# Products of 512 moving columns made as two products of 256, in a two-layer decoder trunk

## The chip, the cores and the metric

The kernel runs on one core of one Trainium2 chip. The metric is the device time of one execution in microseconds (us); the time of a kernel is the median of its runs. TensorE is the engine of the matrix products (PE in the profile, PEld for its weight loads), VectorE is DVE, ScalarE is ACT, GpSimd is POOL and SyncE is SP.

## What is computed

The reference is a trunk of two layers on an input of 256 rows by 2048 columns, all in 32-bit floats. Each layer is a mixer and a squared-ReLU MLP, both behind a norm and with a residual. Cut to what matters here:

```python
D_MODEL, SEQ, DEPTH, D_FF = 2048, 256, 2, 8192
h = x
for layer in range(DEPTH):
    u = rms_norm(h, norm_mix) @ w_in            # 2048 -> 6160 (layer 0) or 7176 (layer 1)
    mix = concat(mixer_a(u), mixer_b(u)) @ w_out    # 2048 -> 2048
    h = h + mix
    h = h + square(relu(rms_norm(h, norm_mlp) @ w_up)) @ w_down   # 2048 -> 8192 -> 2048
return rms_norm(h, final_norm)
```

The mixers (gated linear attention and MoBA in layer 0, FoX and HGRN2 in layer 1) are small beside the four projections.

## The kernel before, in words

Every projection is cut into `Block`s of 1024 output columns (1040 or 1032 in one block of each input projection, `extra` 16 or 8). A block runs over its contraction rows in steps of 128; a step is one unit `i`, with row tile `j` in its block. `fetch` brings the weight rows of a unit by DMA (two units to a transfer of 1 MB), and splits them: ScalarE rounds them to `wh` (line 1001), VectorE makes the remainder `wl` (line 1002). The other operand is split in the same way (`xh`, `xl` for the normed input, `mh`, `ml` for the mixer's output and for the MLP's hidden rows), so each product of the reference is a sum of three: high by high, high by low, low by high.

`step(t, i)` issues the products of unit `i` for the `t`-th half of the 256 rows of x. The main loop issues step 0 of unit `i` and step 1 of unit `i - 2`, and then gives small tasks of the mixers (transposes, scores, attention) a share of the queues by `bg`. A step works in one of two ways:

- Input, output and down projections (line 1045): the stationary operand is a 128x128 piece of `xh`, `xl`, `mh` or `ml`, and the moving operand is a piece of `wh` or `wl`. A block's sums stand in two banks of PSUM of 512 columns each, `acc{t}0` and `acc{t}1` (`b.cuts`). A block with extra columns has cuts of 512 and twice 264 or 260 columns, the last in a bank `aux`. A product is one `matmul` over the columns of one bank.
- Up projections (`turned`, line 1028): the weights are stationary, 128 columns at a time, and the 256 rows of `xh` or `xl` are the moving operand. Two sums of 256 columns stand in one bank, and the flag `start` is given only with the first.

Within a step of the first kind the products go part by part, and in each part bank by bank, so that products next to each other share their stationary operand; in the first and the last step of a block they go bank by bank, so that the first bank is done early and can be read (`b.evac`) while the second is still summed. Each `matmul` of the program becomes a weight load and a product on TensorE, also where the stationary operand is that of the one before. The order on each engine is that of the program except that a scheduler moves instructions a little by what it expects of their times; `pin` holds the first 14 units as written.

Of the kernel before, what the change touches and what calls it, by code (L numbers as in the profile page):

```python
# [38 lines left out]
def trunk(ctx: ExitStack, tc: tile.TileContext, x, ev_norm_mix, ev_w_in, ev_gla_gate_w2, ev_gla_gate_b,  # L39
# [3 lines left out]
    pe, act, dve, pool = nc.tensor, nc.scalar, nc.vector, nc.gpsimd  # L43
# [35 lines left out]
    def until(cond):  # L79
        n = 0  # L80
        while not cond():
            bg(10.0, 10.0)
            n += 1
            assert n < 1000
        state["credit"] = min(state["credit"], 0.0)


    def aux():
        state["aux"] += 1
        return psum.tile([P, 512], F32, name="aux", tag="aux", bufs=NAUX)  # L90

    def aux_done():
        state["aux"] -= 1
# [174 lines left out]
    def pin(op):  # L268

        if state["start"]:  # L270
            tc.keep_in_program_order(op)
# [733 lines left out]
    def step(t, i, end=None):  # L1005

        b, j = units[i]
        n = len(b.rows)
        if not b.ready(j):
            until(lambda: b.ready(j))  # L1010
        if j == 0:
            accs[t] = [psum.tile([P, 512], F32, name=f"acc{t}{c}", tag=f"acc{t}{c}")[:, 0:b.cuts[c][1] - b.cuts[c][0]]
                       for c in range(2)]
            if b.extra:
                accs[t].append(aux()[:, 0:b.cuts[2][1] - b.cuts[2][0]])
        banks = accs[t]
        if b.turned:
            assert end is None
            wh, wl = split[i]
            sh, sl = b.stat(j)  # L1020
            parts = [(wh, sh), (wl, sh), (wh, sl)]
            fs = [(o, k) for o in range(2) for k in range(2)]
            order = [(f, p) for f in fs for p in range(3)] if j in (0, n - 1) else [(f, p) for p in range(3) for f in fs]
            for (o, k), p in order:
                m, a = parts[p]
                c0 = t * 512 + (o * 2 + k) * P

                pe.matmul(banks[o][:, k * S:(k + 1) * S], m[:, c0:c0 + P], a, start=j == 0 and p == 0 and k == 0,  # L1028
                          stop=j == n - 1 and p == 2 and k == 1, skip_group_check=True)
            if j == n - 1:  # L1030
                b.evac(banks, t)
            return
        ts = slice(t * P, (t + 1) * P)
        parts = []
        for ii in range(i, end or i + 1):
            jj = units[ii][1]
            wh, wl = split[ii]
            sh, sl = b.stat(jj)
            parts += [(sh[:, ts], wh, jj == 0, False), (sh[:, ts], wl, False, False), (sl[:, ts], wh, False, jj == n - 1)]
            j = jj  # L1040
        outs = list(zip(banks, b.cuts))

        order = [(o, p) for o in outs for p in parts] if j in (0, n - 1) and i else [(o, p) for p in parts for o in outs]
        for (o, (c0, c1)), (a, m, first, last) in order:
            pin(pe.matmul(o, a, m[:, c0:c1], start=first, stop=last))  # L1045
        if j == n - 1:
            b.evac(banks, t)
            if b.extra:
                aux_done()
# [19 lines left out]
    for i in range(total + LAG):  # L1069
        if i % 2 == 0 and i // 2 + 2 < 8:  # L1070
            load_x(i // 2 + 2)
        if i + AHEAD < total:
            fetch(i + AHEAD)
        state["start"] = i < STARTN
        if i < total:
            step(0, i)
        if i % 2 == 0 and i // 2 + 1 < 8:
            first_norm(i // 2 + 1)
        if i == 4:
            load_vectors()  # L1080
            spawn(vector_task())
            tasks.append(tk_const)
        if i == 12:
            for half in range(2):
                spawn(stats_task("ev_mix", half))
        if LAG <= i < total:
            step(1, i - LAG)
        bg(units[min(i, total - 1)][0].budget)
    step(1, total - LAG, total)
    until(lambda: not tasks)  # L1090

# [29 lines left out]
```

## Time and profile before

| what | value |
|---|---|
| median of 3 runs | 2314.34 us (2314.3 to 2315.16) |
| the profiled execution, its own time | 2313.99 us |
| its span, first to last instruction | 2312.3 us |
| PE busy | 2293.0 us (99% of the span) |
| PEld busy | 2009.5 us (87%) |
| DVE, ACT busy | 1285.3 us (56%), 1086.5 us (47%) |

The span is what the trace shows, and the execution's own time is 1.7 us longer. PE's busy time counts a product from its start to its modelled end, and products overlap, so how fast the products follow each other is read from the distance of their starts, not from the duration of one.

### The profile page before, as it was taken

The page shows a single profiled execution, that of the slowest core. Times are in us where ns is not written, and L with a number is a line of the kernel's source. Part 1 is how long each engine was busy: PE and PEld are TensorE (multiplying, and loading weights), DVE is VectorE, ACT ScalarE, POOL GpSimd, SP SyncE. Part 2 cuts the span into 40 slices and gives each one's busy share as a digit, 9 for nine tenths or more (in the row PEclk, how much of TensorE's full clock was granted, in tenths as well). Part 3 has the DMA queues.
Part 4 walks back from the last instruction along what each step waited for, and adds up shares of the span by engine and source line. Part 5 has one row for each costly group of instructions (what it writes and reads, how often), then busy time and mean ns, then how long its engine had stood idle before and what let it go on. Part 6 is the DMA issues. An engine that isn't in the chain of part 4 may idle for free.

```text
span 2312.3 us, 32691 instructions
## 1 busy us (share of the span) xinstructions
PE 2293.0 (99%) x13652; PEld 2009.5 (87%) x13652; DVE 1285.3 (56%) x1564; ACT 1086.5 (47%) x1370; POOL 62.2 (3%) x136
## 2 busy tenths in 40 slices
PE   8999999999999999999999999999999999999998
PEld 7888888998998998998887888788988988988986
DVE  5575545554554464465557775555554554554554
ACT  5464544443453353354446555544443443443443
POOL 2000100000000000000000000100000000000000
PEclk9999999999999999999999999999999999999999
DMA  7645445555556555555554434455555555565553
GB/s 241 190 155 164 154 156 184 184 198 184 198 185 198 184 198 184 197 186 183 183 181 163 164 128 164 146 182 182 192 192 187 196 187 195 189 194 185 198 185 124
DMA packets 110613, 418.69 MB, mean 181 GB/s; under 512 B 6814, under 2 KB 8944, under 8 KB 110336
## 3 DMA queue, kind: packets, MB, share of 16 engines
q1 hardware_dynamic: 109536, 415.46, 54.5%
q8 instruction: 107, 1.75, 0.3%
q10 hardware_dynamic: 608, 1.06, 0.1%
q14 instruction: 42, 0.34, 0.0%
q0 software_dynamic: 320, 0.07, 0.0%
HBM read 414.47 MB, written 2.10 MB: 180 GB/s over the span
## 4 chain that ended last, share of the span: by engine, by line
PE 97%; ACT 1%; DVE 1%; DMA 0%; SPq 0%; issue 0%; POOL 0%; POOLq 0%; ACTq 0%
PE acc L1045 61%; PE acc L1028 30%; PE aux L438 1%; PE aux L1045 1%; PE aux L277 1%; PE aux L339 1%; DMA raw<-in_ev_w_in_dram 0%; PE aux L516 0%; ACT wh L1001 0%; PE aux L540 0%; DVE wl L1002 0%; PE aux L515 0%; PE aux L431 0%; PE aux L561 0%; PE aux L371 0%; PE aux L560 0%
## 5 line engine op out<-in xcount | busy, mean ns | idle before, releaser
L1002 DVE TENSOR_TENSOR wl<-raw,wh 128x1024 fp32r<-128x1024 f32 (+2 forms) x784 | 960.1, 1226 | 879.4 <-ACT wh L1001 877.3
L1001 ACT ACTIVATE wh<-raw 128x1024 fp32r<-128x1024 f32 (+2 forms) x784 | 830.6, 1061 | 1115.8 <-PE acc L1045 675.2
L1045 PE MATMUL acc<-wh,ml 128*128 128x512 f32 x1280 | 413.7, 394 | 0.0
L1045 PE MATMUL acc<-wl,mh 128*128 128x512 f32 x1280 | 413.0, 393 | 0.0
L1045 PE MATMUL acc<-wh,mh 128*128 128x512 f32 x1280 | 412.6, 393 | 0.0
L1028 PE MATMUL acc<-xh,wh 128*128 128x256 f32 x2048 | 348.8, 277 | 0.0
L1028 PE MATMUL acc<-xl,wh 128*128 128x256 f32 x2048 | 347.9, 277 | 0.0
L1028 PE MATMUL acc<-xh,wl 128*128 128x256 f32 x2048 | 347.9, 277 | 0.0
L1028 PEld LDWEIGHTS acc<-xh,wh 128*128 128x128 f32 x2048 | 287.0, 188 | 2.6
L1045 PEld LDWEIGHTS acc<-wh,ml 128*128 128x128 f32 x1280 | 240.5, 188 | 55.1
L1045 PEld LDWEIGHTS acc<-wl,mh 128*128 128x128 f32 x1280 | 240.4, 188 | 52.7
L1045 PEld LDWEIGHTS acc<-wh,mh 128*128 128x128 f32 x1280 | 238.1, 188 | 55.2 <-DVE stg L897 1.7
L1028 PEld LDWEIGHTS acc<-xh,wl 128*128 128x128 f32 x2048 | 285.2, 188 | 0.7
L1028 PEld LDWEIGHTS acc<-xl,wh 128*128 128x128 f32 x2048 | 285.1, 188 | 0.0
L1045 PE MATMUL acc<-wh,xh 128*128 128x512 f32 x832 | 271.3, 397 | 3.1 <-ACT xh L283 3.1
L1045 PE MATMUL acc<-wl,xh 128*128 128x512 f32 x832 | 262.6, 387 | 2.6 <-DVE wl L1002 2.6
L1045 PE MATMUL acc<-wh,xl 128*128 128x512 f32 x832 | 262.3, 386 | 0.0
L1045 PEld LDWEIGHTS acc<-wl,xh 128*128 128x128 f32 x832 | 152.4, 188 | 34.2 <-DVE wl L1002 4.3
L1045 PEld LDWEIGHTS acc<-wh,xl 128*128 128x128 f32 x832 | 152.8, 188 | 31.0
L1045 PEld LDWEIGHTS acc<-wh,xh 128*128 128x128 f32 x832 | 147.6, 189 | 29.8 <-ACT xh L283 4.0
L872 DVE TENSOR_TENSOR h<-acc,h 128x512 f32<-128x512 f32 x72 | 47.9, 686 | 20.2 <-PE acc L1045 20.2
L897 DVE SCALAR_TENSOR_TENSOR stg<-acc,rrow 128x512 f32<-128x512 f32 x64 | 42.3, 685 | 15.1 <-PE acc L1028 15.1
(241 smaller groups left out, 1005.5 us busy)
## 6 DMA issues: line engine op xcount, KB each, us to landing
raw<-in_ev_w_up_dram SPq DMA_DIRECT2D x64, 1024.0 KB, 5.0
raw<-in_ev_w_down_dram SPq DMA_DIRECT2D x64, 1024.0 KB, 5.5
raw<-in_od_w_up_dram SPq DMA_DIRECT2D x64, 1024.0 KB, 5.0
raw<-in_od_w_down_dram SPq DMA_DIRECT2D x64, 1024.0 KB, 5.5
raw<-in_od_w_in_dram SPq DMA_DIRECT2D x48, 1024.0 KB, 4.9
raw<-in_ev_w_in_dram SPq DMA_DIRECT2D x39, 1024.0 KB, 5.5
raw<-in_ev_w_out_dram SPq DMA_DIRECT2D x16, 1024.0 KB, 5.5
raw<-in_od_w_out_dram SPq DMA_DIRECT2D x16, 1024.0 KB, 5.5
```

The costliest lines, as they stand in the source:

```text
L277: pin(pe.transpose(ps[:, i * 256 + t * P:i * 256 + (t + 1) * P], h[:, t, kt * P:(kt + 1) * P], ident))
L339: pe.transpose(ps[:, i * P:(i + 1) * P], src[:, (n0 + i) * P:(n0 + i + 1) * P], ident)
L438: pe.matmul(ps[:, i * 64:(i + 1) * 64], a, r, start=True, stop=True)
L872: dve.tensor_tensor(h[:, t, sl], acc[i], h[:, t, sl], ALU.add)
L897: dve.scalar_tensor_tensor(y, acc[i].rearrange("p (k s) -> p k s", s=S), 0.0, rr, ALU.max, ALU.mult)
L1001: pin(act.activation(wh, raw, AF.Copy))
L1002: pin(dve.tensor_sub(wl, raw, wh.bitcast(F32)))
L1028: pe.matmul(banks[o][:, k * S:(k + 1) * S], m[:, c0:c0 + P], a, start=j == 0 and p == 0 and k == 0, stop=j == n - 1 and p == 2 and k == 1, ...
L1045: pin(pe.matmul(o, a, m[:, c0:c1], start=first, stop=last))
```

## The change

In `step`, a product whose moving operand has 512 columns is issued as two of 256 columns, with the same stationary operand, next to each other, into the two halves of the same bank. Cuts of 264 and 260 columns stay as they are, and so do the up projections. The flag `start` is given only with the first half of a bank's first product, `stop` only with the last half of its last.

```diff
-        outs = list(zip(banks, b.cuts))
-
-        order = [(o, p) for o in outs for p in parts] if j in (0, n - 1) and i else [(o, p) for p in parts for o in outs]
-        for (o, (c0, c1)), (a, m, first, last) in order:
-            pin(pe.matmul(o, a, m[:, c0:c1], start=first, stop=last))
+
+        outs = [[(o[:, u - c0:v - c0], u, v, u == c0, v == c1) for u, v in
+                 (((c0, c0 + 256), (c0 + 256, c1)) if c1 - c0 == 512 else ((c0, c1),))] for o, (c0, c1) in zip(banks, b.cuts)]
+
+        if j in (0, n - 1) and i:
+            order = [(o, p) for bank in outs for p in parts for o in bank]
+        else:
+            order = [(o, p) for p in parts for bank in outs for o in bank]
+        for (o, u, v, f, e), (a, m, first, last) in order:
+            pin(pe.matmul(o, a, m[:, u:v], start=first and f, stop=last and e, skip_group_check=True))
```

On TensorE, the first step of a block of layer 0's output projection, bank by bank, and the step after it (`mh`, `ml` are the stationary operands; 2646, 2647 and 2718, 2719 are the banks of the two row halves). Before:

```order
1366 L1045 MATMUL acc_2718<-wh,mh_1994 128x512
1367 L1045 MATMUL acc_2718<-wl,mh_1994 128x512
1368 L1045 MATMUL acc_2718<-wh,ml_1995 128x512
1369 L1045 MATMUL acc_2719<-wh,mh_1994 128x512
1370 L1045 MATMUL acc_2719<-wl,mh_1994 128x512
1371 L1045 MATMUL acc_2719<-wh,ml_1995 128x512
1372 L1045 MATMUL acc_2646<-wh,mh_1994 128x512
1373 L1045 MATMUL acc_2647<-wh,mh_1994 128x512
1374 L1045 MATMUL acc_2646<-wl,mh_1994 128x512
1375 L1045 MATMUL acc_2647<-wl,mh_1994 128x512
```

The same place in the changed kernel, where line 1045 has become line 1050:

```order
1367 L1050 MATMUL acc_3792<-wh,mh_2762 128x256 x2
1368 L1050 MATMUL acc_3792<-wl,mh_2762 128x256 x2
1369 L1050 MATMUL acc_3792<-wh,ml_2763 128x256 x2
1370 L1050 MATMUL acc_3793<-wh,mh_2762 128x256 x2
1371 L1050 MATMUL acc_3793<-wl,mh_2762 128x256 x2
1372 L1050 MATMUL acc_3793<-wh,ml_2763 128x256 x2
1373 L1050 MATMUL acc_3690<-wh,mh_2762 128x256 x2
1374 L1050 MATMUL acc_3691<-wh,mh_2762 128x256 x2
1375 L1050 MATMUL acc_3690<-wl,mh_2762 128x256 x2
1376 L1050 MATMUL acc_3691<-wl,mh_2762 128x256 x2
```

Each row has become two products in the same place; nothing stands between the two halves, and the order of banks and parts is the same.

On ScalarE, at the end of the first block of layer 0's input projection (line 628 reads the finished bank `acc_131`, line 1001 rounds weights for later steps). Before:

```order
27 L1001 ACTIVATE wh<-raw 128x1040 x2
28 L628 ACTIVATE stg<-acc_131,rq 128x512
29 L1001 ACTIVATE wh<-raw 128x1040 x2
30 L341 ACTIVATE gqT<-aux 128x4x128
31 L341 ACTIVATE gkT<-aux 128x4x128
```

In the changed kernel:

```order
27 L1001 ACTIVATE wh<-raw 128x1040 x3
28 L628 ACTIVATE stg<-acc_131,rq 128x512
29 L1001 ACTIVATE wh<-raw 128x1040
30 L341 ACTIVATE gqT<-aux 128x4x128
31 L341 ACTIVATE gkT<-aux 128x4x128
```

One rounding of weights has moved ahead of the reading of the bank. Elsewhere on ScalarE and VectorE only single instructions of the mixers and of the weight splits trade places with a neighbour.

## Rows read from the trace of the kernel before

**Rows 1.** The page: span, busy time of each engine, granted clock in 40 slices.

```profile
span 2312.3 us, 32691 instructions
PE 2293.0 (99%) x13652; PEld 2009.5 (87%) x13652; DVE 1285.3 (56%) x1564; ACT 1086.5 (47%) x1370; POOL 62.2 (3%) x136
...
PEclk9999999999999999999999999999999999999999
```

**Rows 2.** The page: the chain that ended last, shares by engine.

```profile
PE 97%; ACT 1%; DVE 1%; DMA 0%; SPq 0%; issue 0%; POOL 0%; POOLq 0%; ACTq 0%
```

**Rows 3.** Waits of PE (what for: us in total, times, longest).

```profile
PE aux L1057 <- DMA vrow<-in_ev_norm_mix_dram: 3.7, 1, 3.7
PE acc L1045 <- ACT xh L283: 3.1, 2, 2.4
PE acc L1045 <- DVE wl L1002: 2.6, 3, 2.2
```

**Rows 4.** Groups of PE's products by form: xcount | busy us, mean ns.

```profile
L1045 PE MATMUL acc<-wh,ml 128*128 128x512 f32 x1280 | 413.7, 394 | 0.0
...
L1028 PE MATMUL acc<-xl,wh 128*128 128x256 f32 x2048 | 347.9, 277 | 0.0
...
L1045 PE MATMUL acc<-wl,xh 128*128 128x512 f32 x768 | 253.5, 395 | 2.6 <-DVE wl L1002 2.6
```

**Rows 5.** Chain in order of time: start us, us, what.

```profile
372.97 38.79 PE acc L1045 x168
...
507.50 83.14 PE acc L1045 x360
...
596.20 82.07 PE acc L1028 x720
```

**Rows 6.** Chain in order of time, among the mixers of layer 1.

```profile
1278.01 1.03 PE aux L438 x8
1279.04 5.59 PE acc L1045 x24
1284.63 0.84 PE aux L438 x8
1285.47 2.83 PE acc L1045 x12
1288.30 0.84 PE aux L438 x8
1289.14 5.60 PE acc L1045 x24
```

**Rows 7.** Timeline of PE, an up projection: start us, us, operation, count.

```profile
596.04 0.63 PE L1028 MATMUL acc<-xh,wh 128*128 128x256 f32 x4
...
598.87 0.63 PE L1028 MATMUL acc<-xh,wh 128*128 128x256 f32 x4
...
604.05 0.63 PE L1028 MATMUL acc<-xl,wh 128*128 128x256 f32 x4
...
604.98 0.62 PE L1028 MATMUL acc<-xh,wl 128*128 128x256 f32 x4
...
610.87 0.39 PE L1028 MATMUL acc<-xl,wh 128*128 128x256 f32 x2
```

**Rows 8.** Timeline of PE, layer 0's block with 264-column cuts.

```profile
66.64 0.28 PE L1045 MATMUL aux<-wh,xh 128*128 128x264 f32 x1
66.77 0.52 PE L1045 MATMUL acc<-wl,xh 128*128 128x512 f32 x2
...
100.39 0.28 PE L1045 MATMUL aux<-wh,xl 128*128 128x264 f32 x1
```

**Rows 9.** Two stretches: length, busy us (count) of each engine, granted clock, DMA.

```profile
520.04:587.04 67.00, 67.00 (x292) 54.43 (x291) 32.30 (x29) 25.46 (x24) 0.00 (x0) 1.00 0.57 189
604.52:660.00 55.48, 55.48 (x491) 55.48 (x490) 29.46 (x28) 26.36 (x29) 0.00 (x0) 1.00 0.56 190
```

**Rows 10.** Timeline of ACT at the end of the first block.

```profile
52.25 2.02 ACT L1001 ACTIVATE wh<-raw 128x1040 fp32r<-128x1040 f32 x2
54.70 0.69 ACT L628 ACTIVATE stg<-acc,rq 128x512 f32<-128x512 f32 x1 [0.43 <-PE acc L1045]
```

**Rows 11.** The page: DMA queue of instructions: packets, MB, share of 16 engines.

```profile
q8 instruction: 107, 1.75, 0.3%
```

## The prediction

> **What bounds the kernel now.** I first read the page's busy times and the chain that ended last. PE is busy 99% of the span, at a granted clock in the top tenth in every slice, the 2.4 GHz level [rows 1], and 97% of the chain is PE [rows 2]. PE's own waits add up to 9.4 us, in six waits [rows 3]. So what counts is how closely PE's products follow each other, and DVE, ACT and the DMA queues matter only where they would make PE wait.
>
> The durations of products say little, since a 512-column product lasts 394 ns and a 256-column one 277 ns [rows 4] while many overlap. I therefore took the chain in order of time, where an undisturbed run of products has a length and a count. In a down projection 360 products of 512 columns take 83.14 us, which is 230.9 ns each; the output projection has the same (38.79 us for 168, 230.9 ns). In an up projection 720 products of 256 columns take 82.07 us, 114.0 ns each [rows 5]. Two of those are 228.0 ns, 2.9 ns less than one of 512. In the input projections, with products of the mixers' small tasks between, 24 products of 512 columns take 5.59 us: 232.9 ns [rows 6].
>
> The timeline of an up projection then shows that 114.0 is a mean over two paces [rows 7]. From 598.87 to 604.05 lie 11 groups of four: 44 products in 5.18 us, 117.7 ns each. From 604.98 to 610.87 lie 13 groups of four: 52 in 5.89 us, 113.3 ns each. The slow pace holds from where the stream of 256-column products begins (596.04; 68 products to 604.05), and from about 604.5 on the fast one holds. Twice the slow pace is 235.4 ns, more than the 230.9 of a product of 512; twice the fast pace is 226.6, less.
>
> **The change part by part.** It takes away 3 x 1280 = 3840 products of 512 columns with `mh` or `ml` (output and down projections) and 3 x 768 = 2304 with `xh` or `xl` (input projections) [rows 4], 6144 in all, and puts 12288 of 256 in their place, each with a weight load of its own.
>
> *Output and down projections, 3840 products.* These run undisturbed for 168 to 360 products at a time [rows 5], so 336 to 720 halves, as long a stream as the up projections have. The nearest row for 256-column products in such a stream is the up projections' mean. 227.97 - 230.94 = -2.97 ns for each product, times 3840: **-11.4 us**. Bounds: the fast pace throughout, -4.3 ns, is -16.5 us; the slow pace throughout, +4.5 ns, is +17.3 us.
>
> *Input projections, 2304 products.* Here small tasks come between after every 12 to 24 products [rows 6], that is 24 to 48 halves, less than the 68 that a fresh stream spent at the slow pace. So I take two thirds of them at the slow pace and one third at the fast: 232.5 ns against the 232.9 of now, -0.4 ns times 2304 = **-0.9 us**. Bounds: all slow +2.5 ns, +5.8 us; all fast -6.3 ns, -14.5 us.
>
> *The weight loads.* They double from 6144 to 12288. At 512 columns PEld is busy 54.43 of 67.00 us, at 256 columns 55.48 of 55.48 [rows 9]. That full share is no bound by itself: eight products of line 438, each with a load of its own and 64 columns, follow each other in 0.84 us [rows 6], so a load can follow a load every 105 ns, below 113.3. Their cost beyond that is in the paces above, and I add nothing. If that cover were gone the pace would be the slow one.
>
> *Instructions.* PE gets 6144 more products and as many loads. The queue that brings instructions is busy 0.3% for 1.75 MB [rows 11], and "issue" is 0% of the chain [rows 2]; nothing is added, behind transfers that run ahead. Doubled, it would still be under 1%.
>
> *Order on the other engines.* At the end of the first block one rounding of weights (2.02 us for two, 1.01 us each) now stands ahead of the reading of the bank by line 628, which before had waited 0.43 us for PE [rows 10]. The reading ends up to 1.0 us later, and the next block's first product needs that bank; transposes that need the read rows stand behind it too. The other trades are of single instructions, with PE not waiting at those places now [rows 3]. I take **+0.5 us**, between 0 and 1.0.
>
> *The end of a block.* Reading the first bank goes beside the second bank's last three products, 0.69 us now and six of 114 ns, 0.68 us, then. Nothing.
>
> Sum: -11.4 - 0.9 + 0.5 = -11.8 us. The profiled execution took 2313.99 us, 1.7 us of it outside the span, and stands 0.35 us below the median. 2313.99 - 11.8 = 2302.2, and with the 0.35 **2302.5 us**, 0.5% faster. What a measurement of this kernel can tell from no change is about 0.2%, 4.6 us.
>
> **The rivals.** *A price for each product (slower).* In the block with 264-column cuts the code of line 1045 already makes two short products with the same stationary operand beside one of 512. From 66.64 to 100.39 lie 71 such sets of three, 33.75 us, 475.4 ns a set [rows 8]. Less 230.9 for the 512 that leaves 122.2 ns for a 264, or 118.5 ns scaled to 256 columns: the slow pace, for 35 us on end. If the split stream behaves like this one, with the moving operand from `wh` and `wl`, and never reaches the fast pace, the 3840 products cost +17.3 us and the 2304 +5.8, together +23.1 (2337 us); with 118.5 for a half it is +6.1 and +4.1 ns, together +32.9 (2347 us). For it speaks that these rows are of the same line and operands. Against it speaks that 512, 264, 264 is an uneven sequence, and the even sequence of the up projections does reach 113.3. It decides as soon as a half takes over 115.5 ns on the mean.
>
> The Trainium skill has a rule that would bring a rise too: "TensorE: Matmul & The Clock Gate", section "Wait — 56ns, not 53.3ns?", says that a product at the full clock costs its columns at 2.4 GHz and about 2.5 ns more whatever its size. By that 6144 more products would cost an estimated 15 us (2330 us). The rows here speak against so simple a sum: it would give 215.8 and 109.2 ns, where the trace has 230.9 and 114.0, so that the excess goes up with the columns more than with the count.
>
> *Only the columns count (no change).* The excess over the columns is proportional to them, and the paces of the split stream mix evenly: a half costs 115.5 ns in the long streams (0 us) and in the input projections 231.0 against 232.9 (-4.4 us). That gives 2310 to 2314. For it speaks that the mean of the two paces is just half of 230.9; against it, that the up projections do not mix evenly but are fast for most of their time (114.0).
>
> *The fast pace everywhere (faster still).* -16.5 - 14.5 = -31.0 us, 2283 us. Against it: the stream of rows 7 begins slow, and small tasks make many new beginnings.
>
> **How the numbers follow.** The forecast, fast for most of the long streams, gets 0.42, with a range of its own from 2294 (long streams all fast, -16.5, and the input projections half and half, 231.0 ns, -4.4) to 2309 (long streams as taken, -11.4, input projections all slow, +5.8). The price for each product gets 0.36, only the columns 0.17, fast everywhere 0.05. The range of 2292 to 2342 leaves out the fast pace everywhere and the upper part of the price, some 0.18 together. Faster by over 0.2%: the forecast and fast everywhere, 0.47. Slower by over 0.2%: the price, 0.36. Within: 0.17.
>
> **What the profile would show.** Right: in the down projections the chain has pieces of 720 halves in about 82 us in place of 83.14 for 360, groups of two starting 227 ns apart after a slow beginning of some 60 to 80 halves; pieces of the input projections with 48 halves at 5.6 us; PEld busy near 100% in both; PE's waits below 12 us in total. Wrong: the same pieces at 84.5 us or more, halves 117 to 119 ns apart to the end of a block, would show the price for each product; a wait of PE on line 628 or 1001 longer than 1 us would show that the order on the other engines matters.

## The result and the profile after

The changed kernel takes 2333.52 us (median of 5 runs, 2332.98 to 2334.82) against 2315.16 for the kernel before beside it (2314.3 to 2316.13): a ratio of 1.0083, interval 1.0071 to 1.0094. That is 18.4 us slower where 11.8 us faster was forecast. The time lies within the stated 2292 to 2342, but on the slower side of no change.

The page of the changed kernel, its rows for [rows 1, 2, 4, 11]:

```profile
span 2333.0 us, 44972 instructions
PE 2314.3 (99%) x19796; PEld 2303.3 (99%) x19796; DVE 1285.5 (55%) x1564; ACT 1087.4 (47%) x1370; POOL 63.6 (3%) x136
...
q8 instruction: 155, 2.54, 0.4%
...
PE 97%; ACT 1%; DVE 1%; DMA 0%; issue 0%; SPq 0%; POOL 0%; POOLq 0%; ACTq 0%
...
L1050 PE MATMUL acc<-wh,mh 128*128 128x256 f32 x2560 | 419.1, 281 | 0.0
```

PE is the bound as before, with 6144 more products. PEld's share rose from 87% to 99%, and "issue" is still 0%. PE's waits, to be read against [rows 3]:

```profile
PE aux L1062 <- DMA vrow<-in_ev_norm_mix_dram: 3.9, 1, 3.9
PE acc L1050 <- ACT xh L283: 2.8, 2, 1.8
PE acc L1050 <- DVE wl L1002: 2.2, 3, 1.8
```

They are 8.9 us, before 9.4. So the time is not in a new wait. It is in the distance of the products, which the chain shows (start us, us, what; to be read against [rows 5, 6]):

```profile
329.46 45.23 PE acc L1050 x384
376.67 39.58 PE acc L1050 x336
...
512.34 84.80 PE acc L1050 x720
602.79 81.87 PE acc L1028 x720
...
1291.93 5.61 PE acc L1050 x48
1302.10 5.71 PE acc L1050 x48
1567.85 38.88 PE acc L1050 x336
2236.77 82.06 PE acc L1050 x702
```

A down projection's 720 halves take 84.80 us, 117.8 ns each, 235.6 ns for what was one product of 230.9. All six pieces of 720 show the same 84.80, and layer 0's output projection has the same pace (45.23 / 384 = 39.58 / 336 = 117.8). The up projections are what they were (81.87 / 720 = 113.7). Layer 1's output projection, at 115.7 (38.88 / 336), and the last down projection, at 116.9 (82.06 / 702), run partly faster. The timeline of PE in the down projection at 512.34:

```profile
520.19 0.63 PE L1050 MATMUL acc<-wh,ml 128*128 128x256 f32 x4
520.66 0.63 PE L1050 MATMUL acc<-wh,mh 128*128 128x256 f32 x4
...
522.54 0.63 PE L1050 MATMUL acc<-wl,mh 128*128 128x256 f32 x4
```

Groups of four start 0.47 us apart, 117.5 ns a half, long after the beginning of the stream at 512.34. In an up projection the slow pace ended after some 70 products [rows 7]; in these six pieces it never ends. In the last down projection both paces take turns from 2279 us on:

```profile
2279.09 0.62 PE L1050 MATMUL acc<-wh,mh 128*128 128x256 f32 x4
...
2281.82 0.63 PE L1050 MATMUL acc<-wh,mh 128*128 128x256 f32 x4
...
2284.65 0.62 PE L1050 MATMUL acc<-wh,mh 128*128 128x256 f32 x4
```

The 24 halves (two steps) from the first row to the second take 2.73 us, those from the second to the third 2.83: the fast pace, then the slow, and so on to the end. The weights' start addresses alternate every two steps as well (below).

### The profile page after: what moved, and what is told of

Same layout as the page of the kernel before. It is cut to its first block, busy times and chain, and to the rows that moved or that the text cites. A ratio compares the mean times of both kernels' runs of the same rounds, so it can differ in the third digit from the quotient of the medians.

```text
span 2333.0 us, 44972 instructions
## 1 busy us (share of the span) xinstructions
PE 2314.3 (99%) x19796; PEld 2303.3 (99%) x19796; DVE 1285.5 (55%) x1564; ACT 1087.4 (47%) x1370; POOL 63.6 (3%) x136
## 3 DMA queue, kind: packets, MB, share of 16 engines
q8 instruction: 155, 2.54, 0.4%
## 4 chain that ended last, share of the span: by engine, by line
PE 97%; ACT 1%; DVE 1%; DMA 0%; issue 0%; SPq 0%; POOL 0%; POOLq 0%; ACTq 0%
PE acc L1050 62%; PE acc L1028 30%; PE aux L438 1%; PE aux L1050 1%; PE aux L277 1%; PE aux L339 1%; DMA raw<-in_ev_w_in_dram 0%; PE aux L516 0%; ACT wh L1001 0%; DVE wl L1002 0%; PE aux L540 0%; DVE hb L741 0%; PE aux L515 0%; PE aux L431 0%; PE aux L562 0%
## 5 line engine op out<-in xcount | busy, mean ns | idle before, releaser
L1050 PE MATMUL acc<-wh,mh 128*128 128x256 f32 x2560 | 419.1, 281 | 0.0
L1050 PE MATMUL acc<-wl,mh 128*128 128x256 f32 x2560 | 418.0, 280 | 0.0
L1050 PE MATMUL acc<-wh,ml 128*128 128x256 f32 x2560 | 417.8, 280 | 0.0
L1050 PEld LDWEIGHTS acc<-wh,ml 128*128 128x128 f32 x2560 | 352.7, 189 | 0.0
L1050 PEld LDWEIGHTS acc<-wh,mh 128*128 128x128 f32 x2560 | 351.4, 188 | 0.0
L1050 PEld LDWEIGHTS acc<-wl,mh 128*128 128x128 f32 x2560 | 351.3, 188 | 0.0
L1050 PE MATMUL acc<-wh,xh 128*128 128x256 f32 (+2 forms) x1600 | 274.7, 287 | 2.8 <-ACT xh L283 2.8
L1050 PE MATMUL acc<-wl,xh 128*128 128x256 f32 (+2 forms) x1600 | 264.5, 281 | 2.2 <-DVE wl L1002 2.2
L1050 PE MATMUL acc<-wh,xl 128*128 128x256 f32 (+2 forms) x1600 | 264.0, 280 | 0.0
L1050 PEld LDWEIGHTS acc<-wh,xh 128*128 128x128 f32 x1600 | 222.5, 190 | 5.5 <-ACT xh L283 3.4
```

The source lines that it names most:

```text
L1050: pin(pe.matmul(o, a, m[:, u:v], start=first and f, stop=last and e, skip_group_check=True))
```

## The experiments

### Each part of the change alone

Which projections pay? The first kernel (f1) splits only the output and down projections (whose blocks have a larger `budget` of small tasks), the second only the input projections.

```diff
-                 (((c0, c0 + 256), (c0 + 256, c1)) if c1 - c0 == 512 else ((c0, c1),))] for o, (c0, c1) in zip(banks, b.cuts)]
+                 (((c0, c0 + 256), (c0 + 256, c1)) if c1 - c0 == 512 and b.budget > 1.5 else ((c0, c1),))] for o, (c0, c1) in zip(banks, b.cuts)]
```

> The changed kernel with only the 3840 products of the output and down projections split, addresses as in the changed kernel: does one part of the change alone. If the slow pace in the long streams is the cause, pieces of 720 halves at 84.8 us and 3840 x (235.6 - 230.9) = +18 us, 2331 to 2334, nearly the whole rise. If the rise comes from the input projections or from the moved instructions on ScalarE and VectorE: below 2320.

Measured: 2328.87 us, 1.0061 (1.0046 to 1.0076), 14.4 us over the 2314.49 of the kernel before beside it. Its down projections have the pieces of the changed kernel (84.80 for 720). It stays under the expected 2331 because a part is not slow: each output projection has a piece of 336 halves in 38.88 us, 115.7 each.

The second (f2) has `b.budget < 1.5` in that place.

> The other part alone: only the 2304 products of the input projections split. If the long streams are the cause: 0 to +3 us, 2314 to 2318. If the small tasks between are: 2325 to 2335.

Measured: 2320.32 us, 1.0025 (1.0015 to 1.0034), 5.8 us. Its chain:

```profile
512.14 83.11 PE acc L1050 x360
...
1195.63 25.04 PE acc L1050 x216
...
1295.52 5.71 PE acc L1050 x48
```

The piece of 216 halves in the kernel before:

```profile
1190.98 24.93 PE acc L1045 x108
```

Down projections keep 230.9 ns a product. In the input projections a piece of 48 halves takes 5.71 us where 24 products took 5.59 [rows 6], 5.0 ns more a product. The longer piece rises by 1.0 ns only, from 230.8 to 231.9: 115.9 ns a half, so a part of these halves has the fast pace. The rise is over the 0 to 3 us expected. The two parts add up (14.4 + 5.8 = 20.2 against 18.4 for both; the medians vary by 1 us).

### Is it the shared stationary operand?

In the split order two halves, or four across banks, have the same stationary operand. Here (f3) the halves go bank by bank with `xh`/`xl` (or `mh`/`ml`) in turn:

```diff
-            order = [(o, p) for p in parts for bank in outs for o in bank]
+            halves = [o for bank in outs for o in bank]
+            order = [(o, parts[k]) for o in halves for k in (0, 2)] + [(o, parts[1]) for o in halves]
```

> The changed kernel with the products of a step in another order: for each half bank xh and xl (mh and ml) in turn, then the products with wl, so that 7 of the 12 halves of a step are followed by one with another stationary operand (in the changed kernel 2 of 12 are). Theory that a load of the same stationary operand right after itself is slow: those halves go at 113 to 114 ns, pieces of 720 at 82.5 to 83.5 us, the whole 2318 to 2326. Theory that any load takes the same and the pace comes from how loads and products stand to each other: 84.8 us and 2331 to 2336, or, if the other order shifts the two against each other, the fast pace in whole blocks.

Measured: 2335.81 us, 1.009 (1.0075 to 1.0105); 720 halves take 84.84 us. With 7 of 12 halves followed by another stationary operand in place of 2, nothing changes: the sharing is not the cause.

### Other sizes of the pieces

Cuts of 320 and 192 columns in place of 256 and 256 (e4, one run):

```diff
-                 (((c0, c0 + 256), (c0 + 256, c1)) if c1 - c0 == 512 else ((c0, c1),))] for o, (c0, c1) in zip(banks, b.cuts)]
+                 (((c0, c0 + 320), (c0 + 320, c1)) if c1 - c0 == 512 else ((c0, c1),))] for o, (c0, c1) in zip(banks, b.cuts)]
```

> The changed kernel with each product of 512 cut at 320 columns (320 and 192) in place of 256, addresses as in the changed kernel. Theory that a weight load sets the pace where the columns are few (a load follows a load at the earliest every 105 to 118 ns): a 192 takes 105 to 118 ns in place of the 85 its columns need, a product 247 to 262 ns, pieces of 360 products 89 to 94 us, the whole 2410 to 2500. Theory of a price of 4.6 ns for each product whatever its size: 235.6 ns as with 256 and 256, pieces of 84.8 us, 2331 to 2336.

Measured: 2483.12 us. In its chain:

```profile
546.94 43.19 PE acc L1050 x336
```

A pair takes 257.1 ns (2 x 128.5), 26 more than one product of 512. In this piece the 192 starts 165 to 171 ns after the 320 (which by the 113.3 of [rows 7] would cost 141.6), and the next 320 only 85 to 92 after the 192. The weight loads start 108 and about 150 ns apart in turn, never less than 108. So something other than the columns sets the distance there.

Four products of 128 columns (e7, one run), the line with 256 in it replaced by

```diff
+                 ([(c0 + k, c0 + k + 128) for k in (0, 128, 256, 384)] if c1 - c0 == 512 else ((c0, c1),))] for o, (c0, c1) in zip(banks, b.cuts)]
```

> The changed kernel with each product of 512 made as four of 128, addresses as in the changed kernel: measures by itself how closely weight loads of the same stationary operand can follow each other, since 128 columns need 53 to 57 ns. Theory that a load sets the pace (from 320 and 192: 257.1 - 141 to 147 = 110 to 116 ns): 110 to 118 ns a quarter, 440 to 471 a product, pieces of a down projection about 158 to 170 us, the whole 3600 to 3800. Theory that the price is 4.6 ns for each product: 4 x (56.7 + 4.6) = 245 ns a product, the whole 2400.

Measured: 3875.38 us. The page's row of the granted clock, and the chain:

```profile
PEclk9995557999999999999999999999999999999999
```

```profile
131.09 35.73 PE acc L1050 x168
...
545.31 71.68 PE acc L1050 x336
...
801.79 85.71 PE acc L1050 x768
...
1065.21 160.75 PE acc L1050 x1440
```

With the granted clock at the 2.4 GHz level 1440 quarters take 160.75 us, 111.6 ns each: half the columns, and only 1.7 ns less than the 113.3 of 256. The weight loads of this piece start 111 to 112 ns apart throughout. So in such a stream the columns no longer set the pace; that the loads do is the likely reading. In three slices and part of a fourth (287 to 622 us) the granted clock was at the 1.2 GHz level, and there a quarter took 213 ns. It took 212.7 in the piece at 131.09 too. The trace's records of the clock begin only at 198.3 us, so the row's first digits are no reading of the clock there.

### Is it where the operands stand in memory?

The up projections have the same size of product and are fast, so I looked at what else differs. A tile of `wh` or `wl` is 1056 columns, 4224 bytes, so consecutive buffers start alternately at 192 and 64 modulo 256; `xh` and `xl` start at 0, `mh` and `ml` at 128 (worked out from the tiles' sizes, not read from a trace). That residue is called the class of a tile below. The idea: the pace hangs on the distance of the classes, moving less stationary operand, modulo 256. The first kernel (e1) pads the weights' tiles to 1088 columns (all start at 192, so the distance is 64 in down and in up projections; one buffer fewer):

```diff
-WB = 1056
+WB = 1088
-    wspl = ctx.enter_context(tc.tile_pool(name="wspl", bufs=6))
+    wspl = ctx.enter_context(tc.tile_pool(name="wspl", bufs=5))
```

> The changed kernel with the weight tiles wh and wl 1088 wide in place of 1056 and five buffers in place of six, so that all of them start at 192 modulo 256 bytes and no longer at 192 and 64 in turn. Theory of the addresses (a stream of 256-column products can reach 113.3 ns only where moving start minus stationary start is 192 modulo 256 bytes): the input projections, 2304 products with xh and xl at 0, have the difference 192 in every step and go to 113.3 to 115 ns a half; output and down projections (mh, ml at 128, difference 64 in every step) stay at 117.8, pieces of 720 halves at 84.8 us. About 10 to 15 us less than the changed kernel's 2333.5, 2318 to 2325. Theory of a price for each product: nothing changes, 2331 to 2336.

Measured: 2356.32 us, 1.0181 (1.0166 to 1.0196). Its chain:

```profile
513.46 84.80 PE acc L1050 x720
603.91 84.80 PE acc L1028 x720
```

Now the up projections, whose code is untouched, have the slow pace from their first product to their last; neither time that was expected came. The same edit to the kernel before (e2):

> The kernel before with the same tiles (1088 wide, five buffers, all at 192 modulo 256). Theory of the addresses: products of 512 take 229.3 ns in every step of the output and down projections (difference 64; pieces of 360 at 82.5 us in place of 83.1) and 233.3 ns in every step of the input projections (difference 192): -6 us and +5 us, 2311 to 2317. It is also the control for five buffers: if PE's waits rise above 20 us in total, the buffers cost time by themselves.

Measured: 2336.17 us, 1.0092 (1.0077 to 1.0107). Its chain:

```profile
509.82 82.47 PE acc L1045 x360
597.90 84.80 PE acc L1028 x720
```

Up projections lose 2.7 us each with nothing split at all (82.07 in [rows 5]), while products of 512 gain a little (229.1 ns). PE's waits are 10.8 us in all, so one buffer fewer costs little by itself; that the addresses act on the pace is shown by e9 below. Next (e3), the split kernel with the same edit and `mh`, `ml` moved to 0, which makes the distance 192 in the down projections and leaves 64 in the up projections:

```diff
+    work.tile([P, 32], F32, name="pad3", tag="pad3")
```

> As the first of these three, with 128 unused bytes ahead of the tiles of mh and ml, which then start at 0 modulo 256: the difference is 192 in every step of all three projections. Theory of the addresses: the split stream reaches 113.3 ns in the long streams; pieces of 720 halves at 81.6 to 82.5 us in place of 84.8, and the whole at 2283 to 2302, faster than both kernels. Theory of a price for each product: the pace stays at 117.8 ns and the time at 2331 to 2336.

Measured: 2334.45 us, 1.0085 (1.0068 to 1.0102). Its chain:

```profile
511.07 81.71 PE acc L1051 x720
598.38 84.80 PE acc L1029 x720
688.75 83.36 PE acc L1051 x720
...
1967.98 81.67 PE acc L1029 x720
```

Here the split halves run at 113.5 ns (81.71 / 720), 227.0 for what was 230.9: the split does not cost anything as such. The time is the one expected of a price for each product (2331 to 2336), but by chance: what the down projections gain the up projections lose; yet one of them, at 1967.98, is fast at the same distance. Other paddings (`pad2` of 24 and `pad3` of 48 columns) put all weights at 0, with distances of 128 in the down and 0 in the up projections (e5):

> The changed kernel with weight tiles 1088 wide, five buffers, all starting at 0 modulo 256, xh and xl at 0, mh and ml at 128: the difference moving minus stationary is 0 in the input and up projections and 128 in the output and down projections, which no kernel so far had. If only the differences 64 and 192 matter by themselves (64 slow, 192 able to be fast), nothing can be said for 0 and 128; if a distance of 192 is the one good value, both go at 117.8 ns a half and the whole takes 2350 to 2360; if any value but 64 is good, both go at 113.3 and the whole takes 2275 to 2295.

Measured: 2394.64 us (one run). Its chain:

```profile
522.91 85.44 PE acc L1051 x720
614.06 86.39 PE acc L1029 x720
```

By the idea 192 is good and 64 bad for halves. The next kernel has 192 for both kinds, with weights at 64, `mh` at 128 and `xh` at 0, and only the long streams split (e8: `pad2` of 40 columns, `pad3` of 32, `WB` and `bufs` as above):

> Weight tiles 1088 wide, five buffers, all at 64 modulo 256; 128 unused bytes ahead of mh and ml, which start at 128; only the products with mh and ml are split, those of the input projections stay at 512. Differences: up projections 192, output and down projections 192 (good for halves), input projections 64 (good for 512). Theory of the addresses: down projections 81.7 us a piece in place of 83.1, up projections 81.6 to 82.0, input products 229.5 to 231 in place of 233: -15, -3 and -6 us, the whole 2288 to 2296, faster than both kernels. If splitting costs by itself: above 2315.

Measured: 2336.19 us, 1.0086 (1.0069 to 1.0103). Its chain:

```profile
509.00 84.80 PE acc L1051 x720
599.39 81.69 PE acc L1029 x720
...
954.84 83.36 PE acc L1029 x720
```

The kernel before, with 192 in its up projections (e9: `pad2`, `WB` and `bufs` the same):

> The kernel before, products of 512 throughout, with weight tiles 1088 wide, five buffers, all at 64 modulo 256, mh and ml at 0, xh and xl at 0: the difference is 64 for all products of 512 (their better value) and 192 for the up projections. Theory of the addresses: down projections 82.5 us a piece, up projections 81.6 to 82.0, input products 229.5 to 231: -7, -3 and -6 us, the whole 2296 to 2304, faster than the kernel before with no product split. If addresses matter only for halves: 2311 to 2317.

Measured: 2311.21 us, 0.9987 (0.9978 to 0.9997). Its chain:

```profile
594.48 83.37 PE acc L1028 x720
...
771.39 81.70 PE acc L1028 x720
```

The idea falls as a full account: the split down projections are slow at the distance that was to be good. And up projections with the same code and classes take 81.7 or 83.4 us, from one block to the next. From e2, with as many buffers, e9 differs by 128 bytes of padding alone, and its up projections take 81.7 or 83.4 us for 84.80, the whole 25 us less: addresses do act on the pace. The same distances on other classes (f4: e8 with `pad` of 56 columns for 24, so that weights and `mh` stand as in e3, `xh` at 128):

> Only output and down projections split; weight tiles 1088 wide, five buffers, at 192 modulo 256, xh and xl at 128, mh and ml at 0: the differences of the run that was to be good everywhere (192 for halves, 64 for products of 512, 192 for the up projections), with the weights and mh, ml at the addresses at which the halves did go at 113.5 ns. If the addresses themselves decide: down projections 81.7 us a piece, 2286 to 2298. If the difference modulo 256 decides and the earlier slow run was of chance: the same. If the pace depends on what came before: either, block by block, between 2286 and 2336.

Measured: 2330.28 us, 1.0069 (1.0052 to 1.0086); 720 halves take 84.80 us, the up projection 81.71. Weights and `mh` stand where e3's halves ran at 113.5, and these run at 117.8. What differs is what came before: there a slow up projection, here a fast one. The class of `xh` differs too, and the input projections are whole here.

### Does the pace depend on what came before?

The new theory: both paces keep themselves in an even stream, and a product of another size can throw the stream from one to the other. Four kernels put such products into the split blocks of f4, one run each; the kernel before beside them took 2314.19 us. First (g1), one row tile in each block, two steps, left at 512 columns:

```diff
-                 (((c0, c0 + 256), (c0 + 256, c1)) if c1 - c0 == 512 and b.budget > 1.5 else ((c0, c1),))] for o, (c0, c1) in zip(banks, b.cuts)]
+                 (((c0, c0 + 256), (c0 + 256, c1)) if c1 - c0 == 512 and b.budget > 1.5 and j != 2 else ((c0, c1),))] for o, (c0, c1) in zip(banks, b.cuts)]
```

> The last version (only output and down projections split, weights at 192, mh and ml at 0, xh and xl at 128 modulo 256) with the products of the third row tile of each split block left at 512 columns. If the pace is set by what came before: some or all blocks change to the fast pace behind that step, pieces near 82 us for 360 products' worth in place of 84.8, the whole 2295 to 2328. If the addresses decide: 117.8 ns a half on both sides of it, 2328 to 2331.

Measured: 2329.98 us; it did not change the pace. Second (g2), the first bank of that row tile cut in 128, 128, 256:

> The same, but in the third row tile of each split block the first bank's products are cut 128, 128 and 256 in place of 256 and 256 (a quarter takes 111.6 ns, so the step is 0.3 us longer). If the pace is set by what came before: blocks change behind that step, 2300 to 2330. If the addresses decide: 2329 to 2334.

Measured: 2323.4 us. The timeline of PE in its first down projection:

```profile
509.87 0.64 PE L1051 MATMUL acc<-wh,mh 128*128 128x256 f32 x4
510.34 0.63 PE L1051 MATMUL acc<-wl,mh 128*128 128x256 f32 x4
...
514.11 0.74 PE L1051 MATMUL acc<-wh,mh 128*128 128x128 f32 x5
...
515.27 0.74 PE L1051 MATMUL acc<-wh,ml 128*128 128x128 f32 x5
...
516.31 0.62 PE L1051 MATMUL acc<-wl,mh 128*128 128x256 f32 x4
...
540.79 0.62 PE L1051 MATMUL acc<-wl,mh 128*128 128x256 f32 x4
...
546.23 0.39 PE L1051 MATMUL acc<-wh,ml 128*128 128x256 f32 x2
546.46 0.46 PE L1051 MATMUL acc<-wh,mh 128*128 128x256 f32 x2
546.76 0.40 PE L1051 MATMUL acc<-wl,mh 128*128 128x256 f32 x2
```

This is the clearest view of all. From 509.87 to 514.11 nine groups of four take 4.24 us, 117.8 ns a half. Then come three groups with quarters, and from 516.31 to 540.79 54 groups take 24.48 us, 113.3 ns a half. Same operands, same code, same clock: behind the quarters the pace is another, and the stream keeps it for 30 us. They are no sure way to the fast one: the row tile's first quarters, at 506.73, have the slow pace behind them.

The fast pace ends at 546.46, with no product of another size. There the second block of the piece begins. The weight load of its first product starts 74 ns after the product before, not 3 or 4 as elsewhere, the second product comes 183 ns after the first, and the 41 halves behind it are 117.8 ns apart. So the fast pace can also end behind a load that comes late. It doesn't always: in h1 below the stream is back at the fast pace a few products after the same event at 545.21, and stays slow after the one at 895.06. VectorE's reading of a bank (line 873) ended at 546.36, 0.06 us before the late load, so the load probably waited for it; that is not shown.

Third (g3), the first bank left at 512 in every fourth row tile (`j % 4 == 2`); fourth (g4), cut in 272 and 240 there.

> The same, with the first bank's products left at 512 in every fourth row tile of the split blocks, four times a block. If the pace is set by what came before and each such step is a new chance: between 2295 and 2330, with blocks that change pace more than once. If the addresses decide: 2327 to 2330.

> The same, with the first bank's products cut 272 and 240 in every fourth row tile of the split blocks. Such a pair shifts products against loads by 16 columns. If the pace is set by what came before: between 2295 and 2330. If the addresses decide: 2328 to 2334.

Measured: 2317.96 and 2311.89 us. In the third the pace changes several times in a block (83.40 us for 675 products); in the fourth 720 products take 82.59 us.

Last, timed in full: 272 and 240 in the first bank of one row tile of each block (h1),

```diff
-                 (((c0, c0 + 256), (c0 + 256, c1)) if c1 - c0 == 512 and b.budget > 1.5 else ((c0, c1),))] for o, (c0, c1) in zip(banks, b.cuts)]
+                 (((c0, c0 + 256), (c0 + 256, c1)) if c1 - c0 == 512 and b.budget > 1.5 and not (j == 2 and c0 == 0) else ((c0, c0 + 272), (c0 + 272, c1)) if j == 2 and c0 == 0 and b.budget > 1.5 else ((c0, c1),))] for o, (c0, c1) in zip(banks, b.cuts)]
```

> The version with the moved tiles and only output and down projections split, with the uneven pair (272 and 240 columns) in the first bank's products of one row tile a block, the third. If the pace is set there and kept: down projections 81.8 to 82.4 us a piece, the whole 2300 to 2310, faster than both kernels. If the pace does not keep and needs the pair anew: 2312 to 2330.

Measured: 2309.76 us, 0.9982 (0.997 to 0.9994), the median of 11 runs from 2305.61 to 2322.1, 20.5 us less than the same kernel without those uneven cuts (f4) and 5.1 us less than the kernel before beside it (2314.83). Its chain:

```profile
506.50 81.93 PE acc L1051 x720
594.08 81.69 PE acc L1029 x720
...
856.34 83.48 PE acc L1051 x720
```

It is the fastest split kernel, but the gain is at the edge of what a measurement can tell, and some blocks still run at a mixed pace (83.48: the piece at 856.34 loses the fast pace at 895.06). The cuts of g4 at the addresses of the changed kernel (h2, input projections whole):

> The changed kernel with its own addresses (distance 64 and 192 in turn), only output and down projections split, and the uneven pair in every fourth row tile. If the pace is set by what came before and the addresses are second: down projections 82.0 to 83.2 us a piece in place of 84.8, the whole 2302 to 2316. If the alternating distance breaks the fast pace again: 2324 to 2330, as with only these two projections split.

Measured: 2328.58 us, 1.0058 (1.0045 to 1.0071); 720 products take 84.46 us. The same cuts gave 2311.89 in g4. With weights that alternate between two classes, uneven cuts alone don't keep the fast pace in the split blocks.

## Why the prediction was wrong

**The step that failed** is the pace of the output and down projections: "The nearest row for 256-column products in such a stream is the up projections' mean", -2.97 ns a product, -11.4 us. The halves ran at the slow pace to the end of nearly every block, +4.6 ns a product; alone that part measured +14.4 us, since a few pieces ran partly faster. The prediction had both paces in [rows 7], and read the slow one as a beginning that any stream leaves after some 70 products. It is a pace of its own: e1's and e2's up projections kept it for 720 products with unchanged code, and the changed kernel's halves for as long. In g2 it ended where products of another size came, and came back at 546.46 without them. [Rows 8], the nearest row by line and operands (118.5 scaled to 256 columns), had shown it for 35 us on end; it was given to the rival.

**Input projections:** -0.9 us was forecast, +5.8 measured. That is the "all slow" bound in number, by luck. About a quarter of the halves there (changed kernel, 110 to 115 ns apart) do follow each other at the fast pace. But the 232.9 that was taken for a product of 512 came from short pieces; in the long piece it is 230.8 and its halves 231.9 (f2), and in short pieces the rise was 5.0 ns. So both the base and the mix were mis-sized.

**Weight loads:** "I add nothing", since a load can follow a load every 105 ns. That row was of other products, with 64 columns. In these streams quarters came every 111.6 ns, so halves at 113.3 have 1.7 ns to spare and not 8. That so small a margin makes two paces possible, because a load that comes late once makes the products behind it late, is argued. The late load in g2 fits it; that the fast pace outlived such a load in h1 does not settle it. The prediction's "if that cover were gone the pace would be the slow one" is what came to pass in size.

**Right were** the instructions (0.4% for 2.54 MB, "issue" 0%), the order on ScalarE (within its 0 to 1.0 us: PE's waits did not grow), the unchanged up projections, and what would show the error: pieces "at 84.5 us or more, halves 117 to 119 ns apart to the end of a block".

**The end of a block** was put at nothing, 0.68 us of products beside 0.69 of reading. At the slow pace, with six halves in 0.71 us, it is: pieces of 84.80 us have no late product. At the fast pace, with 0.68, the next block's first product is followed 70 ns later than others, and in some blocks the fast pace ends behind it (g2, h1).

**The rivals.** The price for each product gave 2337 us by bounds that were the slow pace, 3.5 us above what was measured. Its size holds, its name does not: halves at 113.5 (e3) and the kernel with one uneven step a block (2309.76) show that a second product need not cost anything as such. By the Trainium skill's "TensorE: Matmul & The Clock Gate", section "Wait — 56ns, not 53.3ns?", with its fixed 2.5 ns for each product, an estimated 2330 us would come out, near the 2333.5. The traces don't agree with that reason: e3, e1 and e5 have the same count of products and took 2334 to 2395 us, and f4 and h1, with fewer, 2330 and 2310.

**Open** is what in the chip separates the two paces, and which addresses let a stream reach the fast one. Distances of classes decide neither alone (e8) nor with the absolute classes of both operands (f4 against e3); the changed kernel's up projections keep the fast pace with alternating weights, while its split blocks have it in no steps or, at most, in every other pair of them.

## What to carry to other kernels

Before products are cut, compare a piece's time with the distance at which weight loads follow each other in the same stream (here 113.3 against 111.6 ns): where they nearly met, the pace here went either way for whole blocks. A pace read from another stream, or its mean over two paces, is no price for a new stream; take both paces as cases, and weigh most the row that has the same operands. In such a kernel read the chain's long pieces by length over count after every change, also of streams that the change doesn't touch, since padding of the tiles alone moved them by 3%.

## What the hardware showed that I had not expected

- Two steady paces for the same products at the same granted clock, 113.3 and 117.8 ns for 256 columns, each kept for up to hundreds of products. The pace changed behind products of another size, and the fast one also ended behind a load that came late (g2, h1).
- Start addresses modulo 256 bytes change the pace: up projections 117.8 ns with all weights at 192 and 113.5 or 115.8 with all at 64 (e2, e9), 120.0 at distance 0 (e5); split down projections 118.7 at distance 128 (e5); a product of 512 columns from 230.9 to 229.1 (e2).
- In a stream of products of 128 columns, each with its load, one came every 111.6 ns, and a pair of 320 and 192 took 257.1 ns, 26 more than 512 in one (e4, e7).
- The granted clock fell to the 1.2 GHz level from 287 to 622 us in e7, while PE was busy with products of 128 columns (100% of the span); from 198.3 us to the fall, and behind it, it was at the 2.4 GHz level with PE busy with the same.
